# Moving a chunk pair's transposes and the memory's normalization to later places in an encoder block's order

## The chip, the cores and the metric

The kernel runs on one core of a Trainium2 chip. The metric is the device time of one execution in microseconds (us). The core has five engines with a queue each, worked off in order: TensorE (PE in the profile, its weight loads PEld), VectorE (DVE), ScalarE (ACT), GpSimd (POOL) and SyncE (SP, which here only issues DMAs). Engines wait for each other through semaphores.

## What is computed

One layer of an encoder block on 256 positions of width 1024, all in float32:

```
x <- x + 1/2 * RMSNorm(SwiGLU(RMSNorm(x)))                       first FFN, width 2816
h  = RMSNorm(x); q, forget, input, gates, FoX q, k, v = h @ w_in
A  = HGRN2 gated linear recurrence;  B = forgetting attention
y  = sigmoid(gate_A) * (A @ w_branch_a) + sigmoid(gate_B) * (B @ w_branch_b)
x <- x + RMSNorm(y @ w_out)
x <- x + RMSNorm(CrossAttn(RMSNorm(x), RMSNorm(mem)))            memory of 256 positions, 4 heads
x <- x + 1/2 * RMSNorm(SwiGLU(RMSNorm(x)))                       second FFN
```

with `swiglu(h) = (silu(gate) * up) @ w_down` and `gate, up = split(h @ w_in)`.

## The kernel before

**Numbers.** Every weight and every activation that enters a matmul is split into a high part in TensorE's fast float32r format (a cast on ScalarE, `hi`) and the rest (a subtraction on VectorE, `lo`). A product is three matmuls: high by high, high by low, low by high. So each weight block of 128x1024, a *unit*, costs one DMA into a `raw` buffer (4 of them), one cast (L153, or L173 in `split`) and one subtraction (L155, or L174). The parts lie in 8 `hi` and 8 `lo` buffers.

**Stages.** The first FFN (to about 180 us), the input projections with recurrence and attention, the gates and the two branch products (about 360 to 465 us), the output projection, the cross attention, and the second FFN (from about 585 us). The two halves of 128 positions are called h = 0 and 1.

**An FFN.** The width 2816 is cut into 11 chunks of 256. A chunk's gate and up products go to PSUM; `act_evac` makes `at = silu(gate) * up` (L450 on ScalarE, then L453 or L455 on VectorE). Where positions lie on the partitions (*token-major* chunks, `TOKS`, and pairs, `PAIRS`), TensorE must turn `at` around: `flush(n)` issues four transposes of the oldest chunk in `late` (L445) into a `tr` bank, and a split into `acts`, from which `down` multiplies by w_down (12 matmuls for a chunk and a half).

**Pairs.** At chunks 4, 6, 9 of the first FFN and 3, 6, 9 of the second, `act_pair` computes two chunks together by seven block products instead of eight, from sums of weight blocks (L592) and from five combinations of the input (`de`, `aed`, `baed`, `ad`, `e`), which `pair_inputs` builds once for each FFN (L541 to L544) and splits into `sx` (L173, L174). The products are of 12 matmuls each: `of_x(0)`, de, aed, baed, ad, `of_x(1)` (into a `tr` bank), e. Between them stand `down` products of earlier chunks (`step_between`, in `one`). Two chunks' `at` fall out: chunk c after ad (c, 0 after baed), chunk c+1 after `of_x(1)` and e.

**The gates and branches.** `gates(c)` multiplies and evicts from PSUM on VectorE (L1300), four times two halves; the two banks called `mm` are used in turn. A sigmoid follows, then the branch products: for each column half, branch A times its gate (L1354), branch B times its gate (L1354), and their sum (L1357), transposed by `y_T`. Before the gates' second half the memory `mem` is loaded, the scale of its rows is computed (`rstd_x`), and `row_of` turns that column of numbers into a row spread over all partitions by way of DRAM: a transpose (L360) and two DMAs on GpSimd's queue (L362, L364). L1362 then multiplies the transposed memory by gains and row, eight times, and `split` makes `M`, which the key and value products read later. `mem_sums` makes the same combinations from it (L1408 to L1411).

**What sets the order.** A planner orders each engine's queue. It goes by the order of the code and by its own costs, takes what is ready by these, and prefers what stands in `tc.high_priority()`. `tc.issue_after(i)` lets an engine issue what follows only behind instruction `i` of the same engine: it sets a floor, not a place. `after(n)` uses it with the n-th matmul of `log`, or the last one made so far. `hold` gives a unit's cast and subtraction such floors. Each engine then follows its queue whatever the chip's own times are.

Of the kernel before, what the change touches and what calls it, by code (L numbers as in the profile page):

```python
# [18 lines left out]
P = 128  # L19
# [57 lines left out]
_AT = {}  # L77
# [8 lines left out]
def block_kernel(ctx: ExitStack, tc: tile.TileContext, wts, head_in, gf_in, x_in, mem_in, memT_in, cols, rows, fbias, masks, out):  # L86
# [340 lines left out]
    def ffn(w_in, w_dn, X, r2, n_tok, i_row, first_half, second_half=None):  # L427
# [106 lines left out]
        def pair_inputs():  # L534
            for k in range(2):
              with tc.issue_after(evs[-1][1]):
                V.tensor_tensor(out=xf[k][:, :, P:], in0=xf[k][:, :, P:], in1=bc(row[:, :P], [P, 4, P], 1), op=ALU.mult)
            a, b, d, e = (xf[k][:, :, h * P : h * P + P] for h in range(2) for k in range(2))
            ss = [m4([P, 2, 4, P], n="ss") for _ in range(2)]
            de, aed, ad, baed = (t[:, i] for t in ss for i in range(2))  # L540
            V.tensor_tensor(out=de, in0=d, in1=e, op=ALU.subtract)  # L541
            V.tensor_tensor(out=aed, in0=de, in1=a, op=ALU.subtract)
            V.tensor_tensor(out=ad, in0=a, in1=d, op=ALU.subtract)
            V.tensor_tensor(out=baed, in0=b, in1=aed, op=ALU.add)  # L544
            out = {}
            for n, x in (("de", de), ("aed", aed), ("baed", baed), ("ad", ad), ("e", e)):
                t = m4([P, 2, 4, P], F32R, "sx")
                split(t[:, 0], t[:, 1], x)
                out[n] = t
            return out, q  # L550

        def sum_load(c, n, halves):
            t = []
# [11 lines left out]
                G.dma_start(r, src, accum_op=op)  # L565

        def act_pair(c, between):
            sx, q = pairs_in

            def of(n):  # L570
                return lambda kk: (sx[n][:, 0, kk], sx[n][:, 1, kk])

            def of_x(k):
                return lambda kk: (X.hi(4 * k + kk, 0, P), X.lo(4 * k + kk, 0, P))

            def splits(t):
                u = []
                for r in t:
                    p = parts_of()
                    split(p[0], p[1], r)  # L580
                    u.append(p)
                return u

            def raws(k, n):
                t = [wp.tile([P, D], F32, tag="raw", name=nm("raw"), bufs=4) for _ in range(2)]
                for j in range(2):
                    more(t[j], c, k, n, j, None)
                return t

            def add(t, o):  # L590
                for x, y in zip(t, o):
                    V.tensor_tensor(out=x, in0=x, in1=y, op=ALU.add)  # L592

            def product(ps, stat, u, start):
                for kk in range(4):
                    ah, al = stat(kk)
                    wh, wl = blk(u, kk)
                    for i, (x, y) in enumerate(((ah, wh), (ah, wl), (al, wh))):
                        MM(ps, x, y, start=start and kk == 0 and i == 0, stop=kk == 3 and i == 2, skip_group_check=not start)

            def step_between():
                if between:
                    between.pop(0)()

            def half_tile(n):
                return sp.tile([P, 512], F32, tag="z2", name=nm(n), bufs=3)

            sums, both = sums_of_pair.pop(c)
            copies = [m4([P, 2, 512], n=n) for n in ("vw", "pc")]
            p1, v, w, p5 = (t[:, i] for t in copies for i in range(2))  # L610
            b1 = mm()
            product(b1, of_x(0), splits(sums), True)
            S.copy(p1, b1)
            add(sums, both)
            if c in FETCHED[w_in]:
                for j in range(2):
                    more(both[j], c, 1, 1, j, ALU.add)
            for _ in range(2 if c == 3 else 1):
                step_between()
            b4 = mm()  # L620
            with tc.issue_after(last_silu[0]) if c - 2 in pairs else nullcontext():
                u = splits(sums)
            product(b4, of("de"), u, True)
            S.copy(p5, b4)
            step_between()
            raw = raws(1, 1)
            add(sums, raw)
            product(b1, of("aed"), splits(sums), False)
            S.copy(v, b1)
            step_between()  # L630
            product(b4, of("baed"), splits(raw), False)
            if c not in FETCHED[w_in]:
                add(both, raw)
            with tc.high_priority():
                t = half_tile("c01")
                V.tensor_tensor(out=t, in0=b4, in1=v, op=ALU.subtract)
                act_evac(t, c, 0)
            product(b1, of("ad"), splits(both), False)
            S.copy(w, b1)
            with tc.high_priority():  # L640
                t = half_tile("c11")
                V.tensor_tensor(out=t, in0=p5, in1=w, op=ALU.subtract)
                act_evac(t, c, 1, r2[0], q)
            step_between()
            b0 = trp()
            raw = raws(1, 0)
            m = len(log)
            product(b0, of_x(1), splits(raw), True)
            if late[:1] == [c]:
                flush(m + 10)  # L650
            add(sums, raw)
            with tc.high_priority():
                t = half_tile("c00")
                V.tensor_tensor(out=t, in0=p1, in1=b0, op=ALU.add)
                act_evac(t, c + 1, 0)
            if c + 2 not in pairs and c + 2 < NFF:
                for i in range(1, 4):
                    hold[_AT[w_in] + 4 * (c + 2) + i] = evs[-1]
            step_between()
            product(b1, of("e"), splits(sums), False)  # L660
            with tc.high_priority():
                silu = act_evac(b1, c + 1, 1, r2[0], q)
            last_silu[:] = [silu]
            if c + 1 == NFF - 1:
                table(silu)
            while between:
                step_between()
# [35 lines left out]
        for c in range(n_tok, NFF):  # L703
# [5 lines left out]
            if c in pairs:  # L709
                acts[c + 1] = m4([P, 2, 2, T], F32R, "act")  # L710
                downs = [(i, h) for i in range(done, min(c, NFF - STAG - 1)) for h in range(2)]
                done = max(done, min(c, NFF - STAG - 1))

                def one(i, h):
                    n = len(log)
                    down(i, h)
                    if h == 1 and late[:1] != [c]:
                        flush(n + L_ACT - 12)

                act_pair(c, [lambda i=i, h=h: one(i, h) for i, h in downs])  # L720
            elif c == 2 and first_half:
                n = len(log)
                (outs,) = act_first((c,), mm)
                for h in range(2):
                    flush(n + L_ACT + 24 * h)
                    act_evac(outs[h], c, h)
            elif c in TOKS[w_in]:
                n = len(log)
                wait = 24 if c - 2 in pairs else 0
                for h in range(2):  # L730
                    flush(n + L_ACT + wait + 16 * h)
                    act_tok(c, h)
            else:
                n = len(log)
                up = act_col(c)
                wait = 24 if c - 2 in pairs else 0
                flush(n + L_ACT + wait)
                flush(n + L_ACT + wait + 16)
                split(acts[c][:, 0], acts[c][:, 1], up)
# [593 lines left out]
    def y_T(c, h, m):  # L1333

        tr = trp()
        with after(m):
# [2 lines left out]
            hs = slice(h * P, (h + 1) * P)  # L1339
            split(Y.h[c][:, :, hs], Y.l[c][:, :, hs], tr.rearrange("p (i t) -> p i t", i=4))  # L1340

    for c in range(2):
        for name, X, zc in (("br_a", OA, c), ("br_b", OB, 2 + c)):
            u = chunk(name, c)
            for h in range(2):
                z = zs[zc][:, h]
                m = len(log)
                ps = mm()
                proj_tok(ps, X, u, h)
                if zc != c and h == 1:  # L1350
                    y_T(c, 0, m + L_Y)
                if zc == c and h == 0 and c:
                    y_T(c - 1, 1, m + L_Y)
                V.tensor_tensor(out=z, in0=ps, in1=z, op=ALU.mult)  # L1354
                if zc != c:
                    za = zs[c][:, h]
                    V.tensor_tensor(out=za, in0=za, in1=z, op=ALU.add)  # L1357

    M = Joined()
    for kb in range(KB):  # L1360
        t = memT_s[kb // 4][:, kb % 4]
        V.scalar_tensor_tensor(out=t, in0=t, scalar=cols_s[:, G_KV + kb : G_KV + kb + 1], in1=rowm, op0=ALU.mult, op1=ALU.mult)  # L1362
        evicted.append(split(M.hi(kb), M.lo(kb), t))

    def rows_proj(ps, X, name, h, kbs, cols=(0, 1)):
# [340 lines left out]
```

## Time and profile before

| | us |
|---|---|
| median of three runs | 771.4 (771.38 to 772.7) |
| profiled execution, whole | 778.27 |
| profiled execution, span from first to last instruction | 776.5 |
| TensorE busy | 763.8 |
| VectorE busy | 653.5 |
| ScalarE busy | 514.3 |
| GpSimd busy | 24.5 |
| granted TensorE clock, mean | 0.994 |

The profiled execution is a single one, and stands above the runs without the profiler. In the rows of a time line the first number is the start in us from the span's start, the second the length; then come engine, line, operation, `out<-in` by tile name, shapes and the count of merged instructions. In brackets is the idle time of that engine before it and what ended it. A view of waits gives total, times and longest. Matmul lengths overlap, so the distance between starts tells what one costs. L100 is the helper through which nearly all matmuls go, so that tile names tell them apart.

### The profile page before, as it was taken

How to read it: one execution, taken by the hardware profiler on the slowest of the kernel's cores; microseconds unless marked ns; L12 is line 12 of the kernel's file. 1: busy time of each engine (PE TensorE's matmuls, PEld its weight loads, DVE VectorE, ACT ScalarE, POOL GpSimd, SP SyncE). 2: the span in 40 equal slices, each digit the busy share in tenths (PEclk: the TensorE clock that was granted, in tenths of full speed). 3: DMA queues.
4: the chain of work that ended last, by engine and by line, in shares of the span. 5: the costliest groups of instructions: out<-in, count | busy, mean ns of one | idle time of the engine just before them, and what ended most of it. 6: DMA issues, size and time to landing. Idle time of an engine off the chain costs nothing.

```text
span 776.5 us, 11721 instructions
## 1 busy us (share of the span) xinstructions
PE 763.8 (98%) x4314; PEld 647.3 (83%) x4314; DVE 653.5 (84%) x967; ACT 514.3 (66%) x829; POOL 24.5 (3%) x46
## 2 busy tenths in 40 slices
PE   9999999999999999999998999999999999999996
PEld 8888788888888998898886888888888878888885
DVE  6799998998678998897766857889888999999973
ACT  8676676688675659666674445875868557775762
POOL 0000000000000100200000000001000000000000
PEclk9999999999999999999998999999999999999999
DMA  9768777674744546736566645485385726558341
GB/s 346 231 249 247 213 230 276 184 249 158 245 143 144 183 138 209 253 123 217 156 223 208 200 171 203 144 285 104 118 273 196 252 69 220 214 195 300 104 133 55
DMA packets 45706, 152.65 MB, mean 197 GB/s; under 512 B 5224, under 2 KB 8944, under 8 KB 45648
## 3 DMA queue, kind: packets, MB, share of 16 engines
q1 hardware_dynamic: 43168, 144.83, 54.7%
q0 software_dynamic: 2048, 6.70, 4.6%
q8 instruction: 34, 0.56, 0.3%
q10 hardware_dynamic: 432, 0.37, 0.2%
q14 instruction: 24, 0.20, 0.1%
HBM read 150.81 MB, written 1.06 MB: 196 GB/s over the span
## 4 chain that ended last, share of the span: by engine, by line
PE 65%; issue 15%; DVE 9%; DMA 6%; ACT 4%; POOL 1%; SPq 0%; DVEq 0%; ACTq 0%; POOLq 0%
PE mm L100 31%; PE acc L100 29%; DMA raw<-in_wts_dram 3%; PE tr L100 3%; DVE lo L155 2%; DVE lo L174 2%; DMA sraw<-in_wts_dram 2%; DVE sraw L592 1%; ACT hi L814 1%; PE tr L445 1%; DVE sx L174 1%; PE tr L385 1%; ACT hi L173 1%; ACT hi L153 1%; DMA head<-in_head_dram 1%
## 5 line engine op out<-in xcount | busy, mean ns | idle before, releaser
L155 DVE TENSOR_TENSOR lo<-raw,hi 128x1024 fp32r<-128x1024 f32 (+1 forms) x196 | 231.5, 1199 | 32.2 <-ACT hi L153 27.2
L153 ACT CAST hi<-raw 128x1024 fp32r<-128x1024 f32 (+1 forms) x196 | 198.5, 1033 | 55.5 <-PE mm L100 27.8
L100 PE MATMUL mm<-hi,hlT 128*128 128x512 f32 (+1 forms) x632 | 191.6, 382 | 0.0
L100 PEld LDWEIGHTS mm<-hi,hlT 128*128 128x128 f32 x632 | 117.0, 188 | 20.2
L100 PE MATMUL mm<-lo,hlT 128*128 128x512 f32 (+1 forms) x316 | 119.3, 381 | 0.0
L100 PE MATMUL acc<-hi,act 128*128 128x512 f32 x352 | 113.7, 390 | 0.0
L100 PE MATMUL mm<-hi,sx 128*128 128x512 f32 x280 | 90.6, 391 | 0.0
L173 ACT CAST hi<-sraw 128x1024 fp32r<-128x1024 f32 x70 | 73.0, 1052 | 25.5 <-DVE sraw L592 16.0
L174 DVE TENSOR_TENSOR lo<-sraw,hi 128x1024 fp32r<-128x1024 f32 x70 | 84.2, 1220 | 1.8 <-PE acc L100 0.8
L100 PEld LDWEIGHTS acc<-hi,act 128*128 128x128 f32 x352 | 66.2, 188 | 13.3
L100 PE MATMUL acc<-lo,act 128*128 128x512 f32 x176 | 69.4, 394 | 0.0
L100 PEld LDWEIGHTS mm<-lo,hlT 128*128 128x128 f32 x316 | 59.4, 188 | 9.8
L100 PE MATMUL acc<-hlT,hi 128*128 128x512 f32 x256 | 64.4, 393 | 0.0
L100 PEld LDWEIGHTS mm<-hi,sx 128*128 128x128 f32 x280 | 52.5, 188 | 10.8
L100 PE MATMUL mm<-lo,sx 128*128 128x512 f32 x140 | 54.8, 391 | 0.7 <-DVE lo L174 0.7
L100 PEld LDWEIGHTS acc<-hlT,hi 128*128 128x128 f32 x256 | 46.1, 189 | 8.3
L100 PEld LDWEIGHTS acc<-lo,act 128*128 128x128 f32 x176 | 33.1, 188 | 6.5
L100 PEld LDWEIGHTS acc<-hlT,lo 128*128 128x128 f32 x256 | 35.1, 190 | 2.5
L592 DVE TENSOR_TENSOR sraw<-sraw,raw 128x1024 f32<-128x1024 f32 x30 | 36.0, 1220 | 1.2 <-DMA raw<-in_wts_dram 1.1
L100 PE MATMUL acc<-hlT,lo 128*128 128x256 f32 x256 | 36.2, 283 | 0.0
L174 DVE TENSOR_TENSOR lo<-raw,hi 128x1024 fp32r<-128x1024 f32 x28 | 33.7, 1219 | 0.0
L173 ACT CAST hi<-raw 128x1024 fp32r<-128x1024 f32 x28 | 29.0, 1051 | 5.6 <-issue 3.2
(301 smaller groups left out, 1228.6 us busy)
## 6 DMA issues: line engine op xcount, KB each, us to landing
raw<-in_wts_dram SPq DMA_DIRECT2D x219, 512.0 KB, 4.5
sraw<-in_wts_dram SPq DMA_DIRECT2D x28, 512.0 KB, 6.4
sraw<-in_wts_dram POOLq DMA_DIRECT2D x10, 512.0 KB, 6.1
raw<-in_gf_dram SPq DMA_DIRECT2D x12, 344.0 KB, 3.7
head<-in_head_dram SPq DMA_DIRECT2D x7, 392.0 KB, 6.4
grow<-in_rows_dram SPq DMA_DIRECT2D x4, 512.0 KB, 6.3
xs<-in_x_dram SPq DMA_DIRECT2D x2, 512.0 KB, 7.6
cb<-cd POOLq DMA_DIRECT2D x2, 512.0 KB, 5.4
```

What stands on the lines that cost most here:

```text
L100: log.append(PE.matmul(*args, **kw).ins)
L153: casts.append(S.copy(h, r).ins)
L155: los.append(V.tensor_tensor(out=l, in0=r, in1=h.bitcast(F32), op=ALU.subtract).ins)
L173: a = S.copy(hi, src)
L174: b = V.tensor_tensor(out=lo, in0=src, in1=hi.bitcast(F32), op=ALU.subtract)
L385: PE.transpose(blocks[-1][1], src(kb), ident)
L445: PE.transpose(trv[:, j, h * P : (h + 1) * P], ats[c, h][:, j * P : (j + 1) * P], ident)
L592: V.tensor_tensor(out=x, in0=x, in1=y, op=ALU.add)
L814: S.copy(hi, w)
```

## The change

It has five parts.

- `pair_inputs` splits only de, aed and baed; ad and e are split in the first pair, behind the splits of the weights of the aed product.
- The transposes of a pair's first chunk get a floor 13 matmuls further on: the end of the product or `down` behind `of_x(1)`.
- The transposes of a pair's second chunk move: where the next pair follows at once (chunk 4 to 6 in the first FFN), into that pair's first product; where a token-major chunk follows, behind 17 matmuls of its first half.
- The fourth unit of a token-major chunk behind a pair gets a later floor: behind the evacuation of the pair's last half.
- The eight L1362 get a floor: the first sum of the two gated branches.

```diff
-            for n, x in (("de", de), ("aed", aed), ("baed", baed), ("ad", ad), ("e", e)):
-                t = m4([P, 2, 4, P], F32R, "sx")
-                split(t[:, 0], t[:, 1], x)
-                out[n] = t
-            return out, q
+            def parts(*names):
+                for n, x in (("de", de), ("aed", aed), ("baed", baed), ("ad", ad), ("e", e)):
+                    if n in names:
+                        t = m4([P, 2, 4, P], F32R, "sx")
+                        split(t[:, 0], t[:, 1], x)
+                        out[n] = t
+
+            parts("de", "aed", "baed")
+            return out, q, parts
@@ act_pair
             product(b1, of_x(0), splits(sums), True)
             S.copy(p1, b1)
+            if c - 2 in pairs and late[:1] == [c - 1]:
+                flush(len(log) - 12 + 5)
             add(sums, both)
...
-            product(b1, of("aed"), splits(sums), False)
+            u = splits(sums)
+            if "e" not in sx:
+                more_parts("ad", "e")
+            product(b1, of("aed"), u, False)
...
             product(b0, of_x(1), splits(raw), True)
-            if late[:1] == [c]:
-                flush(m + 10)
...
             step_between()
             product(b1, of("e"), splits(sums), False)
+            if late[:1] == [c]:
+                flush(m + 23)
             with tc.high_priority():
                 silu = act_evac(b1, c + 1, 1, r2[0], q)
             last_silu[:] = [silu]
+            if c + 2 not in pairs and c + 2 < NFF:
+                hold[_AT[w_in] + 4 * (c + 2) + 3] = evs[-1]
@@ ffn
-                    if h == 1 and late[:1] != [c]:
+                    if h == 1 and late[:1] != [c] and (late[:1] != [c + 1] or c + 2 not in pairs):
                         flush(n + L_ACT - 12)
...
                 for h in range(2):
-                    flush(n + L_ACT + wait + 16 * h)
+                    if not wait:
+                        flush(n + L_ACT + 16 * h)
                     act_tok(c, h)
+                    if wait and h == 0:
+                        flush(n + 16)
@@ branches
+    added_z = []
...
-                    V.tensor_tensor(out=za, in0=za, in1=z, op=ALU.add)
+                    added_z.append(V.tensor_tensor(out=za, in0=za, in1=z, op=ALU.add).ins)
...
-        V.scalar_tensor_tensor(out=t, in0=t, scalar=cols_s[:, G_KV + kb : G_KV + kb + 1], in1=rowm, op0=ALU.mult, op1=ALU.mult)
+        with tc.issue_after(added_z[0]):
+            V.scalar_tensor_tensor(out=t, in0=t, scalar=cols_s[:, G_KV + kb : G_KV + kb + 1], in1=rowm, op0=ALU.mult, op1=ALU.mult)
```

More of the change, by code (lines that the diff above doesn't have):

```diff
@@ L567, in act_pair @@
         def act_pair(c, between):
-            sx, q = pairs_in
+            sx, q, more_parts = pairs_in
             def of(n):
```

## The prediction

> **What bounds the kernel now.** I read the page's first block, then TensorE's waits, then the time line around each of them, engine by engine.
>
> ```profile
> span 776.5 us, 11721 instructions
> PE 763.8 (98%) x4314; PEld 647.3 (83%) x4314; DVE 653.5 (84%) x967; ACT 514.3 (66%) x829; POOL 24.5 (3%) x46
> ...
> PE mm L100 <- DVE zg L1300: 2.6, 1, 2.6
> PE tr L445 <- DVE at L455: 1.6, 2, 1.0
> PE tr L100 <- PEq L1695: 0.8, 1, 0.8
> PE mm L100 <- DVE lo L174: 0.7, 1, 0.7
> ```
>
> TensorE is the bound: 763.8 of 776.5 us. A change that leaves its work alone can only remove its waits, all of them short: one at L1300 (the gates), two at L455 (a pair's activations, just before their transposes), one at L174 (a weight's low part). The 0.8 is the start of the kernel.
>
> The largest has a second price, which shows in the time line (start, us, engine, line) and in the stretches behind it (length, then busy us and count of each engine, granted clock before the last two numbers).
>
> ```profile
> 420.24 0.39 PE L100 MATMUL mm<-hi,lT 128*128 128x512 f32 x1
> 423.24 0.79 PE L100 MATMUL mm<-hi,hT 128*128 128x512 f32 x1 [2.61 <-DVE zg L1300]
> ...
> 429.65 0.39 PE L100 MATMUL mm<-hi,hT 128*128 128x512 f32 x1
> 429.88 0.39 PE L100 MATMUL mm<-lo,hT 128*128 128x512 f32 x1
> 423.24:429.65 6.41, 6.41 (x15) 5.01 (x16) 6.34 (x10) 4.41 (x5) 0.00 (x0) 0.52 0.73 248
> 429.65:436.00 6.35, 6.35 (x30) 5.26 (x28) 5.39 (x6) 2.32 (x3) 0.00 (x0) 1.00 0.57 183
> ```
>
> Matmuls of 512 columns start 0.23 us apart at full clock (429.65, 429.88; I use 0.227). From 420.24 to 423.24 are 3.00 us, 2.77 too many. Then 15 matmuls take 6.41 us at clock 0.52 instead of 15 x 0.227 = 3.41: another 3.00. The stall costs 5.77 us, not 2.6.
>
> Its cause is VectorE's order:
>
> ```profile
> 409.99 0.75 DVE L1300 SCALAR_TENSOR_TENSOR zg<-mm,facs,brow 128x512 f32<-128x512 f32 x1
> 418.19 1.28 DVE L1362 SCALAR_TENSOR_TENSOR memT<-memT,cols_s,row 128x256 f32<-128x256 f32 x3 [7.45 <-DMA row<-rd]
> 419.38 1.22 DVE L155 TENSOR_TENSOR lo<-raw,hi 128x1024 fp32r<-128x1024 f32 x1
> ...
> 422.44 0.75 DVE L1300 SCALAR_TENSOR_TENSOR zg<-mm,facs,brow 128x512 f32<-128x512 f32 x1
> ```
>
> The memory's normalization (L1362) stands ahead of the last gate eviction and waits 7.45 us for a row through DRAM. The engine takes its queue in order, so the eviction at 422.44, whose matmuls had long ended (the group after them began 24 x 0.227 = 5.4 us before 420.47, at about 415), stood behind a wait that is not its own. It frees the PSUM bank that TensorE wants at 420.47. Without the wait it runs near 415.3 and ends 4.4 us ahead of that.
>
> **The change part by part.** *The memory behind the first gated branch.* The eight L1362 now follow the first L1357, where the row has long landed. Nothing is added; the stall goes whole: -5.77. The row's two DMAs on POOL's queue and memT's loads on SP's stay where they are. What must hide the eight:
>
> ```profile
> 438.06 0.69 DVE L1357 TENSOR_TENSOR zg<-zg,zg 128x512 f32<-128x512 f32 x1
> ...
> 444.33 0.68 DVE L1354 TENSOR_TENSOR zg<-mm,zg 128x512 f32<-128x512 f32 x1
> 440.00:460.00 20.00, 20.00 (x94) 16.48 (x93) 13.23 (x14) 8.46 (x9) 0.00 (x0) 1.00 0.59 201
> L173 ACT CAST hlT<-memT x8: 402/404/407, 465.8 to 467.9; 128x256 fp32r<-128x256 f32 x8
> ```
>
> Three take 1.28 us, so eight about 8 x 0.4 = 3.4, and the four sums over memT that follow some 2.4 more. VectorE is idle 20 - 13.23 = 6.8 us from 440 to 460, and the normalized memory is first read at 465.8. Queued behind them are the weights' low parts (L155), read a chunk later, and the L1354 of 444.33, which frees a bank that is wanted one group (5.4 us) after its own group's end, so near 449. Issued as one block of 5.8 us from 438.8, with the low parts and copies now between, they would push that L1354 to about 449.5: 0.5 us without cover. The idle row is the nearer one, so I take 0 and keep 0.5.
>
> [...]
>
> *Transposes of a pair's first chunk, 13 matmuls later* (floor m+10 to m+23), *of its second chunk* into the next pair's first product (first FFN) or behind 16 matmuls of the next token-major chunk.
>
> ```profile
> 84.12 0.48 DVE L455 SCALAR_TENSOR_TENSOR at<-c,q,sg 128x256 f32<-128x256 f32 x1
> 93.73 0.48 DVE L455 SCALAR_TENSOR_TENSOR at<-mm,q,sg 128x256 f32<-128x256 f32 x1
> 83.61 0.38 PE L445 MATMUL tr<-ident,at 128*128 128x128 f32 x2
> 84.65 0.44 PE L445 MATMUL tr<-ident,at 128*128 128x128 f32 x2 [0.66 <-DVE at L455]
> 92.92 0.38 PE L445 MATMUL tr<-ident,at 128*128 128x128 f32 x2
> 94.27 0.44 PE L445 MATMUL tr<-ident,at 128*128 128x128 f32 x2 [0.97 <-DVE at L455]
> 663.64 0.40 PE L100 MATMUL mm<-hi,hlT 128*128 128x512 f32 x1
> 664.09 0.44 PE L445 MATMUL tr<-ident,at 128*128 128x128 f32 x2
> ```
>
> An x2 row of 0.38 us holds two transposes that take about 0.22 of the stream (an estimate: the rest overlaps). Start to start, 83.61 to 84.65 is 0.82 too long, 92.92 to 94.27 is 1.13, 663.64 to 664.09 is 0.22: -2.17 where all go. New places: the first, 2.95 us on, finds its input ready since 84.6. The second is due 8 matmuls (1.82 us) later, but TensorE comes 0.82 earlier: 93.14 - 0.82 + 1.82 = 94.14, against an input ready at 94.21; 0.1 stays, and up to 1.2 if L455 slips behind one more low part. The third stands 16 matmuls (3.6 us) behind 664, its input ready at 664.03: 0. The copies on ScalarE and VectorE move along; the activations are next read by a down product at least one pair step (12 matmuls, 2.7 us) later, and their two instructions of about 0.6 us fit. At other pairs the planner had them beyond the floor already, so nothing moves there; 0.
>
> *Parts of "ad" and "e" later.* Second FFN's first pair:
>
> ```profile
> 635.31 1.29 DVE L174 TENSOR_TENSOR sx<-ss,sx 128x512 fp32r<-128x512 f32 x2
> ...
> 637.11 0.69 DVE L174 TENSOR_TENSOR sx<-xf,sx 128x512 fp32r<-128x512 f32 x1
> 637.71 1.23 DVE L592 TENSOR_TENSOR sraw<-sraw,raw 128x1024 f32<-128x1024 f32 x1
> 638.84 2.48 DVE L174 TENSOR_TENSOR lo<-sraw,hi 128x1024 fp32r<-128x1024 f32 x2
> 639.01 0.39 PE L100 MATMUL mm<-hi,sx 128*128 128x512 f32 x1
> 640.13 0.50 PE L100 MATMUL mm<-lo,sx 128*128 128x512 f32 x1 [0.73 <-DVE lo L174]
> 643.52 2.35 DVE L174 TENSOR_TENSOR lo<-sraw,hi 128x1024 fp32r<-128x1024 f32 x2
> 648.42 0.39 PE L100 MATMUL mm<-lo,sx 128*128 128x512 f32 x1
> ```
>
> Two of these sx splits (0.60 each) leave the queue ahead of the low part that TensorE awaits for 0.89 us (639.01 to 640.13, less 0.227). 1.2 us earlier it is in time: -0.89. They come back between there and "ad"'s product near 648.2, whose weights are split from 643.52: 3.7 us ahead of the 648.42 that reads them, so 1.2 fits. ScalarE's two casts likewise. In the first FFN no wait stands there: 0, cover alike.
>
> *The hold on the fourth unit.* Its cast waits for the pair's last SiLU and its low part for L455.
>
> ```profile
> 660.14 3.50 DVE L155 TENSOR_TENSOR lo<-raw,hi 128x1024 fp32r<-128x1024 f32 x3 [0.52 <-ACT hi L153]
> 663.55 0.48 DVE L455 SCALAR_TENSOR_TENSOR at<-mm,q,sg 128x256 f32<-128x256 f32 x1
> 667.35 0.39 PE L100 MATMUL mm<-lo,hlT 128*128 128x512 f32 x1
> ```
>
> The third low part, ended by 663.64, now follows L455 and ends near 665.2, some 2 us before 667.35 reads it. Queued behind the held cast on ScalarE are the next pair's casts, which the planner may send first. The raw buffer comes free about 1.6 us later, and with it SP's next load. I take 0; if that load bound, 1.6 would be its price.
>
> Sum: 5.77 + 2.17 - 0.1 + 0.89 = 8.7; less 0.3 for three new places at the size of the smallest gaps seen (0.1 each): 8.4. The profiled execution took 778.27 (span 776.5, so 1.8 lie around it), 6.9 above the runs' median of 771.4; with 8.4 less it would take 769.9. I carry the 8.4 over to the median: 763.0. [...]
>
> **The rivals.**
> (1) The gate stall goes, but the pairs' gains are eaten, because VectorE is nearly full there (third busy figure):
>
> ```profile
> 640.00:660.00 20.00, 19.87 (x90) 16.47 (x91) 19.59 (x22) 14.75 (x19) 0.00 (x0) 1.00 0.64 213
> ```
>
> 19.59 of 20 us speak for it: an engine this full gives back only what its own gaps hold. Against it, its results still come ahead of their use (3.7 us at 648.42), and the change takes nothing into its queue. 771.4 - 5.8 = 765.6.
> (2) In the timed runs the row lands sooner or the clock does not halve, so less is there to gain: without the slow stretch 8.4 - 3.0 = 5.4, 766.0. For it: 1.13 us of idleness at 94.27 left no slow matmul behind, so the price has a threshold; against it, 2.61 is far beyond. With (1) together, 768.6.
> (3) Slower: "ad" and "e" come too late in the first pair of both FFNs. If the planner puts their casts on ScalarE behind one that waits for its load, which it is free to do, TensorE stalls at "ad"'s product. It decides from 2.6 us on, where the clock halves as at 423: two such stalls at 5.8 are +11.6, 771.4 - 8.7 + 11.6 = 774.3. Against it: 3.7 us of slack on the neighbouring split, and a planner that has their inputs ready from the start.
> (4) The change does not do what it says: a floor only forbids earlier places, and the planner fills the hole that L1362 leaves with something else that waits (a low part whose load is late, a sum of the memory). Then the gate eviction is late again and the transposes may wait at their new places: about 771. Against it: once the row was there, the eviction came within 4.3 us (418.19 to 422.44), with nothing but L1362 and low parts like that of 419.38 in between.
>
> **How the numbers follow.** Forecast 0.62, (1) 0.14, (2) 0.09, (3) 0.09, (4) 0.06. A measurement here tells about 0.2% (1.5 us) from no change. Faster: forecast, (1), (2) = 0.85; same: (4) 0.06; slower: (3) 0.09. Low end: all named waits go (5.77 + 2.17 + 0.89 = 8.83), half the runs' spread (1.3/2) and three more gaps of 0.1 with them, 9.8: 761.6. High end: (1) with (2), 768.6; beyond lie (3) and (4), 0.15.
>
> **What would show it.** Right: no wait at L1300 and granted clock 1.00 through that stage; L1362 behind the first L1357 with no idle before it; TensorE's waits at L445 and in the second FFN's first pair under 0.3 us; span near 768. Wrong: a wait of TensorE over 1 us on sx, on a low part (L155, L174) or on an activation within the pairs, a half clock anywhere between start and end, or VectorE still idle for the row.

## The result, and the profile after

The changed kernel takes 768.96 us, median of 6 runs (768.17 to 769.95). The kernel before, run beside it, takes 771.77 us (771.03 to 773.06). The ratio is 0.9962, with an interval of 0.9949 to 0.9974: faster by 0.38%, 2.8 us. Forecast were 763.0 us and a gain of 8.4, so a third of the gain came.

The profiled executions tell something else. They took 778.27 us before and 769.29 us after: 9.0 us less, and the forecast for this pair of executions was 769.9. In the profile the change did all that was expected of it. First the page and TensorE's waits after:

```profile
span 767.4 us, 11727 instructions
PE 759.8 (99%) x4314; PEld 645.7 (84%) x4314; DVE 652.5 (85%) x967; ACT 513.2 (67%) x829; POOL 24.6 (3%) x46
```

```profile
PE tr L100 <- PEq L1711: 0.8, 1, 0.8
```

TensorE waits once, at the kernel's start. The waits at the gates, at the pairs' activations and at the weight's low part are gone. At the gates (L1300 is L1314 now, L1362 is L1378), the time line shows VectorE, then TensorE, and a stretch shows the clock:

```profile
414.38 0.75 DVE L1314 SCALAR_TENSOR_TENSOR zg<-mm,facs,brow 128x512 f32<-128x512 f32 x1
431.17 1.27 DVE L1378 SCALAR_TENSOR_TENSOR memT<-memT,cols_s,row 128x256 f32<-128x256 f32 x3
```

```profile
413.31 0.39 PE L100 MATMUL mm<-hi,hT 128*128 128x512 f32 x1
418.75 0.39 PE L100 MATMUL mm<-hi,hT 128*128 128x512 f32 x1
```

```profile
420.41:426.80 6.39, 6.39 (x30) 5.30 (x29) 5.09 (x5) 4.16 (x4) 0.00 (x0) 1.00 0.41 121
```

The last gate eviction ends at 415.13, and TensorE opens the next group at 418.75, 24 matmuls behind the group of 413.31 and without a gap. L1378 starts with no idle time ahead of it. The clock stays at 1.00, and 6.39 us hold 30 matmuls (28 begin in them, two lap over from before), where 15 began in 6.41 us. Next the memory by its tile (instructions, least/median/most ns, first and last start), and the transposes with their input:

```profile
L1378 DVE SCALAR_TENSOR_TENSOR memT<-memT,cols_s,row x8: 476/478/480, 431.2 to 440.3; 128x256 f32<-128x256 f32 x8
L173 ACT CAST hlT<-memT x8: 405/408/412, 458.3 to 460.4; 128x256 fp32r<-128x256 f32 x8
```

```profile
86.99 0.60 PE L445 MATMUL tr<-ident,at 128*128 128x128 f32 x4
94.26 0.60 PE L445 MATMUL tr<-ident,at 128*128 128x128 f32 x4
```

```profile
84.03 0.48 DVE L455 SCALAR_TENSOR_TENSOR at<-c,q,sg 128x256 f32<-128x256 f32 x1
93.62 0.48 DVE L455 SCALAR_TENSOR_TENSOR at<-mm,q,sg 128x256 f32<-128x256 f32 x1
```

The normalization spreads over 431 to 440, and ScalarE casts its result from 458 on (only VectorE's four sums over it read it sooner, from 441.28). All four transposes of a chunk now go in one block, 2.5 us and 0.16 us behind the end of their input.

So the mechanism holds, and the question is why the runs show 2.8 of the 9.0 us. The profiled execution after (769.29) lies among the runs of its kernel (768.17 to 769.95). The one before (778.27) lies above all runs of its kernel measured for this case, of which the longest took 776.11.

### The profile page after: what moved, and what is told of

Its sections match the earlier page's. It is cut to its first block, busy times and chain, and to the rows that moved or that the text cites. A ratio compares the mean times of both kernels' runs of the same rounds, so it can differ in the third digit from the quotient of the medians.

```text
span 767.4 us, 11727 instructions
## 1 busy us (share of the span) xinstructions
PE 759.8 (99%) x4314; PEld 645.7 (84%) x4314; DVE 652.5 (85%) x967; ACT 513.2 (67%) x829; POOL 24.6 (3%) x46
## 4 chain that ended last, share of the span: by engine, by line
PE 97%; ACT 1%; issue 1%; DVE 1%; DVEq 0%; ACTq 0%
PE mm L100 49%; PE acc L100 39%; PE tr L100 6%; PE tr L445 1%; PE tr L385 1%; ACT pm L1558 1%; PE tr L1263 0%; PE acc L1571 0%; PE tr L1352 0%; DVE xs L421 0%; ACT L1558 0%; DVE pm L1562 0%; ACT hi L173 0%; DVE post L416 0%; ACT hT L173 0%
```

## The experiments

**Theory A:** the row's landing differs from execution to execution. The profiled execution before was one with a late row, and most runs have less of the gate stall and no half clock. **Theory B**, the rival: every run pays the stall and the half clock, profiled executions of before simply read some 6 us more, and what is lost is the gain at the pairs. In the table are medians of the runs, and ratios to the kernel before on the same chip (before: 771.84 for the first four, 772.04 for the next four, 772.38 for the last two).

| kernel | median us | lowest to highest | ratio, interval |
|---|---|---|---|
| before again | 771.74 | 770.02 to 776.11 | 0.9997 [0.9979, 1.0014] |
| memory edit alone | 770.99 | 769.54 to 771.92 | 0.9982 [0.9967, 0.9996] |
| pair edits alone | 770.11 | 768.49 to 773.70 | 0.9972 [0.9956, 0.9989] |
| transposes alone | 770.69 | 769.04 to 774.10 | 0.9980 [0.9963, 0.9997] |
| row one hop later | 773.94 | 772.37 to 779.02 | 1.0027 [1.0007, 1.0048] |
| row two hops later | 779.21 | 777.10 to 781.07 | 1.0087 [1.0067, 1.0108] |
| after, row two hops later | 768.65 | 768.10 to 768.97 | 0.9952 [0.9938, 0.9966] |
| ad and e alone | 770.45 | 769.96 to 774.54 | 0.9985 [0.9973, 0.9997] |
| after again | 768.47 | 768.08 to 769.22 | 0.9943 [0.9924, 0.9961] |
| after without the hold | 768.59 | 768.30 to 769.74 | 0.9946 [0.9926, 0.9967] |

**The kernel before, profiled again.** No edit.

> The kernel before once more, unchanged. Theory A (the profiled execution of before was one with a late row; most runs have little of its gate stall and no half clock): timed 771 to 773, granted clock 0.997 to 0.999 in most of its runs, its own profile near 770 to 772 with a wait at L1300 well under 2.6 us and clock 0.998. Theory B (the gate stall and the half clock are in every run, and the pairs gave nothing): the profile again near 777 with 2.6 us at L1300, and a clock of 0.994 in the timed runs too. The ratio to the kernel before is 1.000 either way.

> The kernel before, one more profile. Theory A: TensorE's wait at L1300 is what differs from execution to execution; it goes by the row's landing (415.3 in one profile of this kernel with no wait, 418.2 in the other with 2.6), so a span of 769 to 771 where the row lands before 416 and 771 to 777 where it lands later. The pairs' waits at L445 are there in each, 1.0 to 1.7 us together.

> The same once more, with the same expectation: together with the profiles so far it says in how many executions the gate eviction is late, and in how many of these the clock halves (so far once in four executions with a wait of over 1 us and the row in its old place).

The four profiled executions of the same kernel took 778.27, 771.30, 776.07 and 771.97 us. In the first of the new ones the page gives this span, and VectorE's and TensorE's time lines this:

```profile
span 769.5 us, 11721 instructions
```

```profile
415.29 1.28 DVE L1362 SCALAR_TENSOR_TENSOR memT<-memT,cols_s,row 128x256 f32<-128x256 f32 x3 [4.93 <-DMA row<-rd]
419.55 0.75 DVE L1300 SCALAR_TENSOR_TENSOR zg<-mm,facs,brow 128x512 f32<-128x512 f32 x1
```

```profile
420.06 0.39 PE L100 MATMUL mm<-hi,lT 128*128 128x512 f32 x1
420.35 0.50 PE L100 MATMUL mm<-hi,hT 128*128 128x512 f32 x1
```

The row is there at 415.29 instead of 418.19. The eviction follows 4.26 us later and ends at 420.29, and TensorE takes the bank at 420.35, 0.06 us late: in this execution the kernel before stands just at the edge at which the row begins to cost. The eviction stands 4.26 us behind the row's first reader in the other two as well (417.13 to 421.39, 416.37 to 420.63), so what the row loses, the eviction loses. These two executions show 2.06 and 2.40 us:

```profile
422.20 0.50 PE L100 MATMUL mm<-hi,hT 128*128 128x512 f32 x1 [2.06 <-DVE zg L1300]
```

```profile
421.43 0.50 PE L100 MATMUL mm<-hi,hT 128*128 128x512 f32 x1 [2.40 <-DVE zg L1300]
```

Strangely, the shorter wait of 2.06 stands in the longer execution (776.07) and has a half clock behind it; the wait of 2.40 has none, and its execution took 771.97. That is taken up under the clock below. The pairs' waits differ too: at L445 1.6 us, 1.0 and 0.5 in these three, against 1.6 plus the 0.7 on the low part in the profile that the prediction used. My own bounds for these executions were not all met: a row at 416.4 was to give 771 to 777, and gave a span of 770.2; and in that execution the pairs' 0.5 lies under the 1.0 to 1.7 that I expected. Theory B, which wanted 777 each time, is out.

**The memory edit alone.** In before:

```diff
+                    added_z.append(V.tensor_tensor(out=za, in0=za, in1=z, op=ALU.add).ins)
...
+        with tc.issue_after(added_z[0]):
             V.scalar_tensor_tensor(out=t, in0=t, scalar=cols_s[:, G_KV + kb : G_KV + kb + 1], in1=rowm, op0=ALU.mult, op1=ALU.mult)
```

> Before, with the floor for the eight L1362 alone. Theory A: the gate stall is mostly absent from the timed runs, so 0.0 to -1.0 us. Theory B: the stall with its half clock is in every run, -2.8 without the half clock to -5.8 with it. In its profile both expect no wait at L1300 and no half clock; theory A a whole time near 770.5 to 771.5, 3 us (the pairs' waits, 0.82 + 1.13 + 0.22 + 0.89) above the 769.3 of the kernel after less chance.

0.9982 is -1.4 us (-0.3 to -2.5), and -0.85 between medians, against 5.77 in the sum. What changed more is the upper end: 771.92, where the kernel before reaches 776.03 beside it. The long runs went. That they are the runs with the stall and the half clock fits the two long profiled executions (778.27 and 776.07), but a run without a trace does not show its waits, and a wait at full clock can stand near the median (2.40 us in the execution of 771.97). Theory A fits: the interval leaves out theory B's 2.8 to 5.8, and by the ratio the gain is a little more than A's 1.0. The edit's own profile, 769.54, lies under the 770.5 to 771.5 expected; the pairs' waits at L445 were 0.6 us in it.

**The pair edits alone.** After, with L1362 at its old place:

```diff
-        with tc.issue_after(added_z[0]):
-            V.scalar_tensor_tensor(out=t, in0=t, scalar=cols_s[:, G_KV + kb : G_KV + kb + 1], in1=rowm, op0=ALU.mult, op1=ALU.mult)
+        V.scalar_tensor_tensor(out=t, in0=t, scalar=cols_s[:, G_KV + kb : G_KV + kb + 1], in1=rowm, op0=ALU.mult, op1=ALU.mult)
```

> After, with the eight L1362 put back to their old place: the four edits on the pairs alone. Theory A: -2.0 to -3.1 us (0.82 + 1.13 + 0.22 + 0.89), nearly all that the whole change gave (-2.8). Theory B: 0 to -0.5, since the pairs' waits are taken back by a full VectorE. If the row happens to be late in its profiled execution, a wait at L1300 is there again.

-2.2 us by the ratio (-0.9 to -3.4), -1.7 between medians; the upper end is 773.70. The gain at the pairs is real and was not eaten. Together the two halves give 1.4 + 2.2 = 3.6 us, and the whole change measured 2.9 by the first ratio (0.0038 x 771.8) and 4.4 by the second (0.0057 x 772.4): they add up.

**The pair edits apart.** The transposes alone (the floors of the `flush` calls as in the change, nothing else), and the parts of ad and e alone:

```diff
-            if late[:1] == [c]:
-                flush(m + 10)
...
+            if late[:1] == [c]:
+                flush(m + 23)
```

> Before, with the two moves of the pairs' transposes alone. Theory A: -2.0 us (0.82 + 1.13 + 0.22, less 0.1) and TensorE's two waits at L445 gone, the 0.7 us wait on a low part near 640 still there. Theory B: 0 to -0.5.

```diff
+            u = splits(sums)
+            if "e" not in sx:
+                more_parts("ad", "e")
-            product(b1, of("aed"), splits(sums), False)
+            product(b1, of("aed"), u, False)
```

> Before, with the parts of ad and e made later and nothing else. The prediction's term: -0.89. Theory A: the wait before it was 0.73 in two traces and absent in two others, so -0.3 to -0.6 us on the mean. Rival (3), that ad and e come late: a wait of TensorE on sx near 642 and a slower time.

-1.5 us and -1.2 us. Both are gains of the size of their waits, within intervals of about 1 us to each side; the second is above the 0.3 to 0.6 expected. The profile with the transposes alone did not come out as expected: one wait at L445 stayed, at the second chunk's new place (94.14, its last two transposes at 94.96), and the gate wait stands in it, too:

```profile
PE mm L100 <- DVE zg L1305: 1.7, 1, 1.7
PE tr L445 <- DVE at L455: 0.4, 1, 0.4
```

So that place is a narrow one: 0.16 us to spare in the profile after, 0.44 us short in this one. In the profile with ad and e alone TensorE has no wait on the low part and none on sx, so the rival that ad and e come too late (3) did not happen:

```profile
PE mm L100 <- DVE zg L1307: 3.2, 1, 3.2
PE tr L445 <- DVE at L455: 1.4, 2, 0.8
PE tr L100 <- PEq L1702: 0.8, 1, 0.8
PE acc L100 <- ACT hi L821: 0.3, 1, 0.3
```

It also holds the longest gate wait seen with the row's own two DMAs, 3.2 us (L1307 is L1300 there). Seven profiled executions now have L1362 and the row in their old place: four of before, and one each with the pair edits, the transposes, and ad and e alone. Their gate waits are 2.61, 0.06, 2.06, 2.40, none, 1.68 and 3.24 us, 1.7 in the mean, and the clock halves in two of them. So the wait is there in most of these executions; what is rarer is the half clock. The 1.7 lies well within the interval of the memory edit alone (0.3 to 2.5).

**The row made later.** In before, with the last gate eviction held behind five of the L1362, so that it cannot slip ahead, and one or two copies more through DRAM:

```diff
+        for _ in range(far):
+            rd, near = dp.tile([n, 4, 32], F32, name=nm("rd")), rd
+            G.dma_start(rd, near)
         G.dma_start(row[:, : n * P], rd.rearrange("h k t -> (h k t)").partition_broadcast(P))
...
+                with tc.issue_after(i.ins):
+                    V.scalar_tensor_tensor(out=z[:, h], in0=ps, scalar=r2[h], in1=brow, op0=ALU.mult, op1=ALU.add)
...
-    rowm = row_of(fac[1])
+    rowm = row_of(fac[1], far=1)
```

> Before, with one more copy of the 1 KB through DRAM ahead of the broadcast, and the last gate eviction held behind five of the L1362 so that it cannot slip ahead. In the traces so far a hop takes 3.3 to 3.6 us, and the eviction here comes 2.0 us behind the row instead of 4.25. Theory A (the price of the gate stall goes by how late the row is, with 3 us more only once the clock halves): in the traces of before the stall was 0 to 2.6, so here 1 to 4, and in some of the runs the half clock on top: 773 to 777, median about +3.5. Theory B (every run of before pays the stall and the half clock): +1.3, the added lateness alone.

> The same with two more copies. Theory A: a stall of 4.5 to 8 us in every run, with a half clock in every run: +4 more than with one hop from the hop and the rest of the 3 us, 779 to 782, +8 to +10; the profile shows a wait at the gate eviction of over 4 us and the granted clock near 0.5 behind it. Theory B: +5.

+1.9 us and +7.2 us between medians, so the second hop cost 5.3. One hop was to cost about 3.5 by theory A and 1.3 by theory B; its interval, 0.5 to 3.7, holds both. In its profile the wait at the gate is 1.1 us, since the eviction stands only 2 us behind the row here. The runs with one hop fall into two groups: six from 772.4 to 774.4 with a mean granted clock of 0.997 to 0.999, and four from 776.1 to 779.0 with 0.994 to 0.996. By that clock the half clock is in some runs and not in others, with the same program. With two hops the wait is 7.6 us, and the clock is at 0.50 from 422.94 to 433.18 (below). A later row costs more, as theory A says; its sizes were too large, by 1.6 us for one hop and about 1 for two (+8 to +10). The likely reason, not shown by itself, is that the kernel before has some stall in its median already.

The same two copies in after:

> After, with two more copies of the row through DRAM. The row landed near 414 in its traces and is first read at 431; two hops take about 7 us more: 421. Both theories: no change against after (-2.8 us to before), no wait of VectorE on the row. If something else than the lateness of the row slows the stage, it should be slower.

768.65 us: nothing lost. In VectorE's time line the normalization starts at 430.67 with no idle time ahead of it, though GpSimd issues the broadcast 8.1 us later (418.71 against 410.65):

```profile
430.67 1.27 DVE L1381 SCALAR_TENSOR_TENSOR memT<-memT,cols_s,row 128x256 f32<-128x256 f32 x3
```

This is what the memory edit buys: not a fixed 5.8 us, but that the time no longer depends on the row.

**After again, and after without the hold.**

```diff
-            if c + 2 not in pairs and c + 2 < NFF:
-                hold[_AT[w_in] + 4 * (c + 2) + 3] = evs[-1]
```

> The kernel after once more, to have it on one chip with the next. Theory A: -3.0 us against the kernel before (the memory edit alone gave -0.9, the pairs alone -1.7 between medians), 768.2 to 770.5 with no run above 771: the long runs of before (to 776) are those with the late row.

> After, without the hold on the fourth unit of a chunk behind a pair. The prediction's term for it is 0 (price of 1.6 if SP's next load bound). If it is 0: the same as after within 0.5 us. If the hold helps: L455 waits behind low parts again, a wait at L445 near 660 of 0.2 to 1 us and as much slower than after. If the hold costs: faster than after by up to 1.6.

The two are equal within 0.15 us, and the profile without the hold has no wait at L445 either. The hold is worth nothing that these runs can tell. No version beat after.

## Why the prediction was wrong

**The step that failed is "I carry the 8.4 over to the median."** The sum was made of waits of one execution, and that execution was the longest of its kernel that was seen. Its 6.9 us above the median were not a constant that stands beside every profile: they were for the greater part the very waits that the sum counts. The four profiled executions of before bear this out: TensorE's waits behind the kernel's start add up to 4.9, 1.8, 4.1 and 2.9 us, and the spans are 9.1, 2.1, 6.9 and 2.8 us above after's 767.4; the first and third, where the waits alone fall short, are the two with a half clock. After's profiled execution, without those waits, stands inside its own runs: 769.29 among 768.17 to 769.95, so between the two figures that I compared there is no such constant. That nothing of the gain would be lost between them was my assumption, and no run shows it.

Point by point:

- *The gate stall with the half clock, 5.77.* Mechanism right (VectorE's order, the row, the bank), and gone in every profile with the edit. As a term for the median it was mis-sized: 1.4 by the ratio of the edit alone. In four profiled executions of before the wait was 2.61 with 6.83 us of half clock (2.77 + 3.00 in the sum), 0.06, 2.06 with 3.42 us of half clock, and 2.40 without any.
- *The transposes, 2.17 - 0.1.* 1.5 measured alone. No wait is left at 94.26 in the profile after, but 0.44 us were left there with the transposes alone, between the 0.1 that the sum gave this place and the 1.2 that it named as possible. The places came out as worked out (94.26 against a forecast 94.14).
- *The parts of ad and e, 0.89.* 1.2 measured alone, with an interval of 0.2 to 2.1. In two of four profiles of before that wait is absent; in the first and the third it was 0.7 and 0.3. So this term, too, stood on one execution.
- *The hold, 0.* Right, as far as 768.47 with it and 768.59 without can tell.
- *The memory behind the first branch takes nothing from cover, 0 (bound 0.5).* Right: no wait of TensorE from 413 on, and ScalarE's casts begin 17 us behind the last L1378.
- *Rival (2)*, "the row lands sooner or the clock does not halve", came nearest to what happened. It was given 0.09 and was priced wrongly: I took only the slow stretch out of the gain (8.4 - 3.0 = 5.4). If the row lands sooner, the stall goes as well: 8.4 - 5.77 = 2.6, and 771.4 - 2.6 = 768.8, against 768.96 measured. That it comes so near is partly luck: the memory edit alone gained 1.4, not 0, and the pair edits 2.2, not 2.6. My reason against it, that 2.61 us is far beyond a threshold for the clock, does not hold either: the clock stayed at 1.00 with waits of 2.40 and 3.24 us and halved with one of 2.06 (below). Rival (3)'s "from 2.6 us on" fails by the same 3.24 us.
- *Rivals (1), (3), (4)* did not happen: the pairs' gain arrived for the greater part (2.2 of 3.0), ad and e are in time, the planner put nothing that waits into the hole.
- *What would show it*: each sign of "right" is in the profile after, with a span of 767.4. The profile could not show that the median would not follow; only runs of both halves could.

That the runs of before scatter up to 776 and those of after do not was the clue that the three runs first shown (771.38, 771.4, 772.7) were too few to give. Whether being profiled makes a late row more likely stays open: the profiled execution was the shortest of its series with the memory edit alone, the pair edits alone and one hop, and the longest with ad and e alone and with two hops.

## What to carry to other kernels

Ahead of taking a wait's length from a profile into a forecast, compare that execution with the runs: where it is longer than they are, suspect its waits, here above all the one for the row's DMAs: a gain that removes them may belong to that execution and not to the median. The wait for this chain of small DMAs differed from execution to execution (VectorE's wait at L1362 was 7.45, 4.93, 6.85 and 7.23 us in the four profiles of before); price such a wait by several profiles, or by making the transfer one and two hops later and reading the slope. Moving such a consumer to where the row has long been there also takes the long runs away: 768.1 to 770.0 after, 770.0 to 776.1 before.

## What the runs showed of the hardware

**The length of a wait alone does not decide whether the clock halves.** In the profile of before the clock falls at 422.62 and is back at 429.45, in the execution with the 2.06 us wait at 423.34 and 426.76, with two hops at 422.94 and 433.18: 6.83, 3.42 and 10.24 us at half clock. The stretches on both sides of these changes show it (length, then busy us and count of PE, PEld, DVE, ACT, POOL, granted clock, DMA share, GB/s), first before:

```profile
419.21:422.62 3.41, 1.42 (x7) 0.84 (x5) 3.41 (x6) 0.00 (x0) 0.00 (x0) 1.00 0.28 77
422.62:426.04 3.42, 2.80 (x7) 2.22 (x8) 3.42 (x5) 2.54 (x3) 0.00 (x0) 0.50 0.79 261
426.04:429.45 3.41, 3.41 (x10) 2.63 (x9) 3.34 (x7) 1.69 (x2) 0.00 (x0) 0.50 0.76 279
429.45:432.86 3.41, 3.41 (x17) 2.82 (x16) 3.41 (x4) 2.39 (x3) 0.00 (x0) 1.00 0.24 61
```

the execution of before with the 2.06 us wait:

```profile
419.93:423.34 3.41, 1.35 (x6) 0.97 (x6) 3.41 (x6) 1.16 (x2) 0.00 (x0) 1.00 0.75 183
423.34:426.76 3.42, 3.42 (x10) 2.64 (x9) 3.38 (x6) 2.32 (x3) 0.00 (x0) 0.50 0.82 266
426.76:430.17 3.41, 3.41 (x16) 2.78 (x16) 3.38 (x6) 2.56 (x3) 0.00 (x0) 1.00 0.42 166
```

the kernel with ad and e alone, whose wait of 3.24 us ends at 422.38:

```profile
419.00:422.30 3.30, 0.14 (x1) 0.00 (x0) 3.30 (x6) 0.00 (x0) 0.00 (x0) 1.00 0.47 154
...
417.12:420.53 3.41, 2.02 (x9) 1.32 (x8) 3.21 (x6) 0.00 (x0) 0.00 (x0) 1.00 0.01 2
420.53:423.95 3.42, 1.57 (x7) 1.31 (x8) 3.42 (x5) 1.58 (x2) 0.00 (x0) 1.00 0.70 242
423.95:427.36 3.41, 3.41 (x17) 2.83 (x16) 3.38 (x7) 2.86 (x4) 0.00 (x0) 1.00 0.82 287
```

the execution of before with the 2.40 us wait, which ends at 421.43:

```profile
417.11:420.52 3.41, 1.92 (x9) 1.27 (x7) 3.41 (x6) 0.00 (x0) 0.00 (x0) 1.00 0.23 47
420.52:423.94 3.42, 2.51 (x11) 2.08 (x12) 3.42 (x5) 2.51 (x4) 0.00 (x0) 1.00 0.80 258
423.94:427.35 3.41, 3.41 (x17) 2.77 (x16) 3.38 (x7) 2.88 (x4) 0.00 (x0) 1.00 0.89 305
```

and the kernel with two hops, whose wait was 7.61:

```profile
419.53:422.94 3.41, 1.14 (x6) 0.59 (x4) 0.00 (x0) 0.00 (x0) 1.06 (x2) 1.00 0.33 134
422.94:426.35 3.41, 0.00 (x0) 0.00 (x0) 0.86 (x3) 0.00 (x0) 0.00 (x0) 0.50 0.19 38
426.35:429.77 3.42, 1.49 (x4) 1.21 (x5) 3.42 (x8) 1.51 (x2) 0.00 (x0) 0.50 0.01 2
429.77:433.18 3.41, 3.41 (x10) 2.65 (x9) 3.41 (x7) 2.08 (x3) 0.00 (x0) 0.50 0.47 154
433.18:436.60 3.42, 3.42 (x17) 2.81 (x16) 2.78 (x4) 2.33 (x3) 0.00 (x0) 1.00 0.43 134
```

Subtract the first busy figure from the length: in the 3.41 us ahead of each fall TensorE was idle for 1.99, 2.06 and 2.27 us (its ends in a trace are modelled). With the 3.24 us wait it was idle for 3.16 us of the 3.30 from 419.00 to 422.30, and the clock stayed at 1.00 there and behind it, to 427.36. So waits of 2.40 and 3.24 us cost their own length alone, and waits of 2.06, 2.61 and 7.61 us a half clock besides; what decides it, these runs do not show. In each of the three that halved the clock TensorE was busy throughout the last 3.41 or 3.42 us of half clock (3.41 us with the 2.61 us wait, 3.42 with the 2.06, 3.41 with the 7.61), and behind them the clock is at 1.00. In such a stretch 8 matmuls of 512 columns begin in place of 15: in the first profile of before their starts are 0.43 us apart, against 0.227 at full clock. The counts in the rows are higher, since they take in what laps over an edge.

**The row's way through DRAM is not one duration.** From the issue of the broadcast to the start of L1362 it took 4.98 us in the first profile of before (413.21 to 418.19) and 3.40 in the second (411.89 to 415.29). Another 1.36 us of the difference was there when the way began: the transpose of the scale came 1.36 us later (408.73 against 407.37), as did the scale's first step, which follows ScalarE's sums over the memory (L275: 401.93 against 400.57). 1.58 and 1.36 make up the 2.90 us by which L1362 started later, to 0.04 us.
